# The last phase of a seven-product down projection divided in two, with late tiles from a ring of their own

## The chip, the cores and the metric

The kernel runs on one core of a Trainium2 chip. A core has five engines that run their own instruction lists and meet by semaphores: TensorE (PE, matrix products), VectorE (DVE), ScalarE (ACT), GpSimd (POOL) and SyncE (SP, which here only issues transfers). Sixteen DMA engines move data. The metric is the device time of one launch in microseconds (us).

## The reference, cut to what matters

One decoder layer on 512 tokens of width 1024, in fp32: two causal attention branches on a modulated input, merged by gates, an output projection and a layer norm, then a gated feed-forward part with a causal convolution of width 3 and a second layer norm.

```python
mod = c @ w_ada + b_ada
sh1, sc1, gt1, sh2, sc2, gt2 = [m[:, None, :] for m in jnp.split(mod, N_MOD, axis=-1)]
u = x * (1.0 + sc1) + sh1
proj = u @ w_in                      # q, k, v of both branches, forget logits, two gates
...
merged = jax.nn.sigmoid(g_a) * (y_fox @ w_fox_proj) + jax.nn.sigmoid(g_b) * (y_sb @ w_sb_proj)
x = _layer_norm(DEEPNORM_ALPHA * x + (1.0 + gt1) * (merged @ w_o), ln1_g, ln1_b)
u2 = x * (1.0 + sc2) + sh2
h = _causal_depthwise_conv(u2 @ w_up, conv_w, conv_b)      # 1024 -> 2 x 2816
h_gate, h_val = jnp.split(h, 2, axis=-1)
ffn_out = (jax.nn.silu(h_gate) * h_val) @ w_down           # 2816 -> 1024
x = _layer_norm(DEEPNORM_ALPHA * x + (1.0 + gt2) * ffn_out, ln2_g, ln2_b)
```

## The kernel before, in words

**Arithmetic.** Each fp32 product is three matmuls: weights and activations are split into a high half (rounded, by ScalarE, `hi_of`) and a low half (the rest, by VectorE, `lo_of`, the helper line L88), and high x high, high x low and low x high are added in a PSUM bank (`mm3`, L126 to L128, and `product`, L1040 to L1042). There are eight banks of 128x512.

**Weights.** A list `items` holds every weight tile in the order of use. `weights(i)` issues loads in this order on SP into a ring `raw` of five tiles of 128x1024, and calls the splitting of an item two ahead of its use. SP's list is in program order, so a load that waits for a free tile or for data holds up all loads behind it. The order of the other engines' lists is set by a scheduler from the program's order and its own estimate of when things are ready. Tiles that are kept for long (activations' halves `hv`, held weights `wdh`, `wdl`) come from a ring `z` of 58 tiles of 128x512.

**Before the feed-forward part.** While attention and merge run, the modulation vectors that are still missing are made on the side (`add_ada`, a tile of `w_ada` or `w_ct` at a time: the operations `ac` on VectorE, `raw,modr<-raw,cbc` and a reduction). The tiles of the output projection are scaled by `gt1` on GpSimd (L617). Then the output projection runs block by block (four blocks of 128 tokens): matmuls, the norm (`o_norm`, with a load of the input rows into `xn`, L874) and four transposes per block (`o_turn`, L902).

**The up-projection** has 44 column groups `n` of 128 columns, 24 matmuls each; each group is evacuated by ScalarE and VectorE through the convolution (`cv`). Two groups of gate and two of value make a pair `p`; there are eleven pairs.

**The down projection** splits tokens in two halves (blocks 0, 1 and blocks 2, 3), the 2816 rows into pairs, and the 1024 columns in two, and forms the four quadrants from seven products instead of eight, with sums of weight blocks and of activation blocks. Three products per pair (Y, Z2, P1; `early_products`, 18 matmuls) run while the up-projection goes on; for them `pair_proc` adds weight blocks, one addition by an accumulating transfer on the GpSimd queue (L148). One such sum is written to DRAM (`t13`) by the ScalarE queue, to be read again later. The other four products run behind the up-projection over all pairs: phase Z (right half of `t13`), phase V (left half), and a last phase with X (weights B21, columns 1536 to 2047 of the packed pair) and W (weights B22 times 1 + gate, columns 1024 to 1535). Combinations of the banks, a product with the gate (`gated`, L1113, L1114), and the second layer norm follow (`tail`: statistics, first pass L1128, second pass L1132, output).

**The last phase before:** for pairs 0 to 4, X and W take turns from one tile of 128x1024. The last six pairs (LATE = 6) have held tiles: scaled B22, written to DRAM as `wgt` between groups 36 and 41 (`scale_proc`), and B21, loaded together into a tile of the `raw` ring in phases Z and V and split into four held tiles. Blocks 0 and 1 are normed while X and W of the other blocks run (`first_rows`), then block 2, then block 3 in two pieces of 256 columns. The rows of the second norm's scale and shift are loaded on the GpSimd queue in phase V.

Of the kernel before, what the change touches and what calls it, by code (L numbers as in the profile page):

```python
# [8 lines left out]
F32 = mybir.dt.float32  # L9
F32R = mybir.dt.float32r  # L10
BF16 = mybir.dt.bfloat16
# [5 lines left out]
P = 128  # L17
# [22 lines left out]
LATE = 6  # L40
EARLY = 2
GS = 9
# [7 lines left out]
def layer_kernel(ctx: ExitStack, tc: tile.TileContext, out, xT, x, cT, crow, wa0, wa1, bcol, bgt, w1, wct, wv, bf,  # L50
# [7 lines left out]
    wgt = [tc.dram_tile([P, 512], F32, name=f"wgt_{q}") for q in range(LATE)]  # L58
    stg = ctx.enter_context(tc.tile_pool(name="stg", bufs=1))
    pp = ctx.enter_context(tc.tile_pool(name="pp", bufs=8, space=PSUM))  # L60
    zp = ctx.enter_context(tc.tile_pool(name="zp", bufs=1))
    st0 = ExitStack()
# [27 lines left out]
    cbc = const([P, D], F32, "cbc")  # L90
# [18 lines left out]
    identb = const([P, P], BF16, "identb")  # L109
    V.tensor_copy(identb, ident)  # L110
    zerob = const([P, P], BF16, "zerob")
    G.memset(zerob, 0.0)
    mska = const([P, P], BF16, "mska")
    G.affine_select(mska, zerob, pattern=[[-1, P]], compare_op=ALU.is_ge, fill=NEG, base=0, channel_multiplier=1)
    dg = const([P, 512], F32, "dg")
# [22 lines left out]
    def weights(i, ahead=AHEAD):  # L138
        while state["load"] < min(len(items), i + LOADS):
            it = items[state["load"]]  # L140
            it[3] = stg.tile([P, 1024], F32, name=nm("raw"), tag="raw", bufs=LOADS)
            c = 0
            for src in it[0] if isinstance(it[0], list) else [it[0]]:
                w = src.shape[-1]
                nc.sync.dma_start(it[3][:, c : c + w], src)
# [481 lines left out]
    def scale_proc(q):  # L627
        def f(r):
            V.tensor_tensor(r[:, 0:512], r[:, 0:512], gt[1][:, 512:1024], ALU.mult)
            G.dma_start(wgt[q], r[:, 0:512])  # L630
        return f

# [186 lines left out]
    fill(1 << 30)  # L819
    st2.close()  # L820


    st3 = ExitStack()
# [103 lines left out]
    def pair_proc(p):  # L927
        def f(r):
            b = items[pi[p][0]][4]
            V.tensor_tensor(r[:, 0:512], r[:, 0:512], b[:, 0:512], ALU.add)  # L930
# [9 lines left out]
    def add_pair_items(p):  # L940
        pi.append([add_item(wdp[p][:, 0:1024], raw_proc)])
        items[-1].append(wdp[p][:, 512:1536])
        pi[p].append(add_item(wdp[p][:, 0:512], halves_proc, 512))
# [4 lines left out]
    for n in range(2 * FT):  # L948
        wui.append(add_item(wup[n], split_proc))
        if n >= 5 and n % 4 == 1 and n < 2 * FT - 2:  # L950
            add_pair_items((n - 5) // 4)
        if n >= 6 and n % 4 == 2:
            add_pair_sums((n - 6) // 4)
        if 0 <= n - 2 * FT + LATE + 2 < LATE:
            q = n - 2 * FT + LATE + 2
            add_item(wdp[FP - LATE + q][:, 1024:1536], scale_proc(q), 512)
    zi, vi, cli, ci = [], [], [], []

    def add_late():
        if len(cli) < LATE:  # L960
            q = len(cli)
            cli.append(add_item([wgt[q], wdp[FP - LATE + q][:, 1536:2048]], wdc_proc))

    for n, half in (zi, 512), (vi, 0):
        for p in range(0, FP, 2):
            ws = [t13[q][:, half : half + 512] for q in range(p, min(p + 2, FP))]
            n.append(add_item(ws, split_cols(512 * len(ws)), 512 * len(ws)))
            if half and p == 2:
                add_pair_items(FP - 1)
                add_pair_sums(FP - 1)  # L970
            if not half or p == 8:
                add_late()
    for p in range(FP - LATE):
        ci.append(add_item(wdp[p][:, 1024:2048], split_proc))
# [7 lines left out]
    weights(last_wo, 0)  # L982
# [79 lines left out]
    hc = []  # L1062
    for n in range(2 * FT):
        if n < NSPLIT:
            h, l = items[wui[n]][4]
            ps = bks[n]
            up_mm(ps, h, l, slice(256, 512))
        else:
            ps = bank()
            h, l = weights(wui[n], min(LOADS - 1, wui[min(n + 2, 2 * FT - 1)] - wui[n]))  # L1070
            up_mm(ps, h, l, slice(0, 512))
            if n % 2 == 0 and 6 <= n < 22:
                o_x1((n - 6) // 4, n // 2 % 2 == 0)
            if n >= 7 and n % 4 == 3:
                early_products((n - 7) // 4)
            if n in (3, 4):
                list(ada_split(n + 3, 0))
            if n in (4, 5):
                list(ada_sum(n + 2))
# [23 lines left out]
    def fine(s):  # L1103
        return fin.tile([P, 512], F32, name=nm(s), tag="fz", bufs=12)

    r = x1
# [9 lines left out]

    wc = {}
# [19 lines left out]
    def t_phase(ps, idx, half, mark):  # L1137
        for n, k in enumerate(idx):
            w = weights(k)
            for p in range(2 * n, 2 * n + 2):  # L1140
                if half == 0 and GS <= p < FP:
                    ready(p)
            for a in range(2):
                p = 2 * n + a
                if p < FP:
                    t = ops[p][2][half]
                    for i in range(2):
                        m = product(ps[i], t[:, top[i]], t[:, bot[i]], *([v[:, a * 512 : (a + 1) * 512] for v in w]), p == 0, p == FP - 1)
                    ops[p][2][half] = None
            mark(n, m)  # L1150

    def z_mark(n, m):
# [3 lines left out]
        if n == 2:  # L1156
            early_products(FP - 1)
            Y, Z2, P1 = yz
# [5 lines left out]
        if n in (3, 4):  # L1164
            gated(n - 1, 0, p1[n - 3], p1[n - 3])

    def v_mark(n, m):
# [8 lines left out]
        if n == 2:  # L1176
            for i in range(2):
                t = fin.tile([P, D], F32, name=f"ln2_{i}", tag=f"ln2_{i}")
                paced(G.dma_start(t, lnrow[2 + i : 3 + i, :].broadcast_to([P, D])), m)
                lnr.append(t)  # L1180
        if n == 5:
            S.activation(lnr[0], lnr[0], AF.Copy, scale=-0.5)

    lnr = []
    Z = [bank() for _ in range(2)]
    t_phase(Z, zi, 0, z_mark)
    W = [bank() for _ in range(2)]
    t_phase(W, vi, 1, v_mark)
    for i in range(2):
        V.tensor_tensor(c22[i], u3[i], W[i], ALU.add)  # L1190
        V.tensor_tensor(u2[i], u2[i], W[i], ALU.add)
    for i in range(2):
        gated(i, 1, c22[i], c22[i], ALU.subtract)
    X, W = [[bank() for _ in range(2)] for _ in range(2)]
# [7 lines left out]
    for p in range(FP - LATE):  # L1202
        o, sp = ops[p][1], ops[p][3]
        w = weights(ci[p])
        for i in range(2):
            product(X[i], o[:, top[i]], o[:, bot[i]], *half(w, 1), p == 0, False)
        for i in range(2):
            product(W[i], sp[:, top[i]], sp[:, bot[i]], *half(w, 0), p == 0, p == FP - LATE - 1)
        if p % 2 == 0 and p < 4:
            first_rows(p // 2)  # L1210
    for q in range(LATE):
        wc[q] = weights(cli[q])
    for i in range(2):
        V.tensor_tensor(u2[i], W[i], u2[i], ALU.subtract)
        gated(2 + i, 1, u2[i], u2[i])
    for i in range(2):
        st = stat_tile()
        pieces = [(0, 0, 512), (1, 0, 512)] if i == 0 else [(0, 0, 512), (1, 0, 256), (1, 256, 512)]
        for n, (e, c0, c1) in enumerate(pieces):
            ps = bank()[:, 0 : c1 - c0] if e else X[i]  # L1220
            for q in range(LATE):
                t = ops[FP - LATE + q][3 if e else 1]
                product(ps, t[:, top[i]], t[:, bot[i]], wc[q][0][1 - e][:, c0:c1], wc[q][1][1 - e][:, c0:c1], e == 1 and q == 0, q == LATE - 1)
            v = r[2 + i][e][:, c0:c1]
            if e:
                V.tensor_tensor(v, v, ps, ALU.add)
            else:
                gated(2 + i, 0, p1[i], ps)
            V.bn_stats(st[:, n, :], v)
        tail(2 + i, st, pieces, nc.sync)  # L1230
# [71 lines left out]
```

## Time and profile before

| | us |
|---|---|
| runs shown | 765.49, 765.67, 760.73 (median 765.49) |
| the profiled execution | 761.97 |
| its span, first to last instruction | 760.2 |
| PE busy in the span | 736.8 |
| VectorE busy | 608.6 |
| ScalarE busy | 382.9 |
| up-projection, 420 to 640: PE busy | 220.00 of 220 |
| phases Z, V, X and W, 674 to 752: PE waits | 6.2 |
| from PE's last matmul to the end of the span | 8.4 |

How to read it: times are microseconds from the span's start. A line such as `L88 DVE ... wl<-raw,wh` names the line of the kernel, the engine, the operation and the tile written and read, without buffer numbers. `[0.76 <-DVE wl L88]` or "PE ps L1041 <- DVE wl L88: 5.8, 7, 1.2" tells that PE's instruction of line 1041 waited for VectorE's of line 88, 5.8 us in total, seven times, 1.2 at most. Durations overlap a little: the start of the next instruction is the better measure of what one costs. The granted clock was 0.995.

### The profile page before, as it was taken

How to read it: one execution, taken by the hardware profiler on the slowest of the kernel's cores; microseconds unless marked ns; L12 is line 12 of the kernel's file. 1: busy time of each engine (PE TensorE's matmuls, PEld its weight loads, DVE VectorE, ACT ScalarE, POOL GpSimd, SP SyncE). 2: the span in 40 equal slices, each digit the busy share in tenths (PEclk: the TensorE clock that was granted, in tenths of full speed). 3: DMA queues.
4: the chain of work that ended last, by engine and by line, in shares of the span. 5: the costliest groups of instructions: out<-in, count | busy, mean ns of one | idle time of the engine just before them, and what ended most of it. 6: DMA issues, size and time to landing. Idle time of an engine off the chain costs nothing.

```text
span 760.2 us, 9892 instructions
## 1 busy us (share of the span) xinstructions
PE 736.8 (97%) x3472; PEld 608.6 (80%) x3472; DVE 608.6 (80%) x1016; ACT 382.9 (50%) x679; POOL 113.7 (15%) x144
## 2 busy tenths in 40 slices
PE   8999999989999999999999999999999999999795
PEld 4878888867888887888889888888888888887574
DVE  6869799888898799666576999776867777679797
ACT  4567466675876564335045644543455344446520
POOL 1035223343000012453000000000000000000010
PEclk9999999999999999999999999999999999999998
DMA  8954446334532255435052656654764576767812
GB/s 332 405 193 132 173 173 216 111 112 139 167 121 76 84 166 193 145 111 191 3 152 84 207 183 192 208 142 157 210 186 139 170 213 221 226 179 258 278 53 77
DMA packets 42564, 128.80 MB, mean 169 GB/s; under 512 B 5617, under 2 KB 6129, under 8 KB 42514
## 3 DMA queue, kind: packets, MB, share of 16 engines
q1 hardware_dynamic: 37458, 112.61, 44.3%
q0 software_dynamic: 3184, 9.51, 5.8%
q10 hardware_dynamic: 1872, 6.05, 2.1%
q8 instruction: 27, 0.44, 0.2%
q14 instruction: 23, 0.19, 0.1%
HBM read 118.64 MB, written 9.44 MB: 168 GB/s over the span
## 4 chain that ended last, share of the span: by engine, by line
PE 71%; DVE 15%; DMA 6%; issue 4%; ACT 3%; DVEq 0%; SPq 0%; ACTq 0%
PE ps L126 15%; PE ps L127 15%; PE ps L128 15%; PE ps L286 5%; DVE wl L88 3%; PE ps L1041 3%; PE ps L1042 3%; PE ps L1040 3%; PE ps L880 2%; PE ps L881 2%; PE ps L879 2%; DMA raw<-in_wa 2%; DVE ac L571 2%; DVE om L498 2%; DVE raw L186 1%
## 5 line engine op out<-in xcount | busy, mean ns | idle before, releaser
L168 ACT ACTIVATE wh<-raw 128x1024 fp32r<-128x1024 f32 (+1 forms) x102 | 107.0, 1050 | 145.8 <-PE ps L127 97.9
L88 DVE TENSOR_TENSOR wl<-raw,wh 128x1024 fp32r<-128x1024 f32 (+2 forms) x111 | 132.5, 1195 | 42.0 <-ACT wh L168 41.7
L126 PE MATMUL ps<-u2h,wh 128*128 128x512 f32 (+1 forms) x376 | 141.5, 376 | 0.1
L128 PE MATMUL ps<-u2h,wl 128*128 128x512 f32 (+1 forms) x376 | 141.2, 376 | 0.0
L127 PE MATMUL ps<-u2l,wh 128*128 128x512 f32 (+1 forms) x376 | 141.2, 376 | 0.0
L126 PEld LDWEIGHTS ps<-u2h,wh 128*128 128x128 f32 x376 | 70.8, 188 | 13.2 <-issue 0.5
L127 PEld LDWEIGHTS ps<-u2l,wh 128*128 128x128 f32 x376 | 70.8, 188 | 12.9
L128 PEld LDWEIGHTS ps<-u2h,wl 128*128 128x128 f32 x376 | 70.8, 188 | 12.7
L126 PE MATMUL ps<-uh,wh 128*128 128x512 f32 x200 | 79.5, 397 | 0.0
L127 PE MATMUL ps<-ul,wh 128*128 128x512 f32 x200 | 78.2, 391 | 0.0
L128 PE MATMUL ps<-uh,wl 128*128 128x512 f32 x200 | 78.1, 390 | 0.0
L148 POOL DMA_DIRECT2D raw<-in_wdp x11 | 9.6, 870 | 248.8 <-DMA raw<-in_wdp 151.9
L128 PEld LDWEIGHTS ps<-uh,wl 128*128 128x128 f32 x200 | 37.6, 188 | 8.2
L499 POOL TENSOR_TENSOR pt<-pt,om 128x127 f32<-128x127 f32 (+3 forms) x32 | 42.7, 1346 | 9.4 <-DVE om L498 9.4
L126 PEld LDWEIGHTS ps<-uh,wh 128*128 128x128 f32 x200 | 37.6, 188 | 7.3
L127 PEld LDWEIGHTS ps<-ul,wh 128*128 128x128 f32 x200 | 37.7, 188 | 7.1
L1082 ACT ACTIVATE cv<-ps,cw 128x512 f32<-128x512 f32 x44 | 33.6, 764 | 7.2 <-PE ps L128 3.9
L1083 DVE SCALAR_TENSOR_TENSOR cv<-ps,cw,cv 128x511 f32<-128x511 f32 x44 | 32.8, 745 | 4.0 <-ACT cv L1082 3.9
L88 DVE TENSOR_TENSOR wdl<-raw,wdh 128x512 fp32r<-128x512 f32 x45 | 30.8, 687 | 6.0 <-ACT wdh L638 5.9
L1084 DVE SCALAR_TENSOR_TENSOR cv<-ps,cw,cv 128x510 f32<-128x510 f32 x44 | 32.8, 746 | 0.5
L617 POOL TENSOR_TENSOR raw<-raw,gt 128x1024 f32<-128x1024 f32 x8 | 20.7, 2590 | 79.7 <-DMA raw<-in_wo 74.2
L1090 ACT ACTIVATE cv<-cv 128x512 f32<-128x512 f32 x22 | 13.9, 633 | 36.4 <-DVE cv L1084 34.9
(223 smaller groups left out, 1621.3 us busy)
## 6 DMA issues: line engine op xcount, KB each, us to landing
raw<-in_wup SPq DMA_DIRECT2D x44, 512.0 KB, 3.5
raw<-in_wa SPq DMA_DIRECT2D x32, 512.0 KB, 3.9
raw<-in_wdp SPq DMA_DIRECT2D x27, 512.0 KB, 4.9
raw<-in_wct SPq DMA_DIRECT2D x25, 512.0 KB, 3.3
wa<-in_wa SPq DMA_DIRECT2D x14, 512.0 KB, 7.9
raw<-in_wdp SPq DMA_DIRECT2D x23, 256.0 KB, 4.9
raw<-in_wdp POOLq DMA_DIRECT2D x11, 512.0 KB, 6.6
t<-raw ACTq DMA_DIRECT2D x11, 512.0 KB, 5.1
```

Source lines behind the costliest of these rows:

```text
L88: return V.tensor_tensor(o, i, fl(hi), ALU.subtract)
L126: PE.matmul(ps, wh, ah, start=first, stop=False)
L127: PE.matmul(ps, wh, al, start=False, stop=False)
L128: return PE.matmul(ps, wl, ah, start=False, stop=last)
L168: state["hi"] = S.activation(h[:, 0:cols], r[:, 0:cols], AF.Copy)
L286: PE.matmul(grp[g], w, u, start=j == 0 and n == 0, stop=j == KT - 1 and n == (1 if g == 7 else 2))
L499: G.tensor_tensor(pt[b][:, s : e - 1], pt[b][:, s : e - 1], om[:, s + 1 : e], ALU.mult)
L1040: PE.matmul(ps, ah, bh, start=first, stop=False)
L1041: PE.matmul(ps, ah, bl, start=False, stop=False)
L1082: S.activation(t, ps, AF.Identity, bias=cw[:, n, 3:4], scale=cw[:, n, 2:3])
L1083: V.scalar_tensor_tensor(t[:, 1:], ps[:, 0:511], cw[:, n, 1:2], t[:, 1:], ALU.mult, ALU.add)
L1084: V.scalar_tensor_tensor(t[:, 2:], ps[:, 0:510], cw[:, n, 0:1], t[:, 2:], ALU.mult, ALU.add)
```

## The change

- **The last phase is two phases.** X (B21) runs for all eleven pairs as a phase of its own, two pairs to a tile of 128x1024, loaded from the weights. Then W (B22) runs: three pairs from tiles of `wgt`, then eight held pairs (LATE = 8).
- **All of B22 is scaled in the up-projection.** `pair_proc` multiplies it by the gate into a tile `wg` (VectorE) and writes it to DRAM on the ScalarE queue. `scale_proc` is gone.
- **Held tiles have their own ring:** the eight late tiles of `wgt` load into a ring `rl` of four tiles of 128x512, and the loads are spread over phases V and X.
- **Statistics earlier:** the result of X for blocks 2 and 3 is gated and added as W begins, and the statistics of its columns are taken there.
- **The second norm's rows** are loaded by SP at group 24, and one is scaled at group 28.
- **Modulation tiles:** in the merge, `add_ada` runs for j of 3 and above in the one list and for every j in the other, so the last ones come later; the sums of groups 6 and 7 are done at n = 3 and 4.
- **The first loads of the up-projection:** `weights(last_wo, 0)` is called ahead of the point where the up-projection's items are added to the list.
- Some constants move into a pool that closes after the merge, and Z's combinations come one step later.

```diff
-LATE = 6
+LATE = 8
...
+            if it[2] == 512:
+                it[3] = state["late"].tile([P, 512], F32, name=nm("rl"), tag="rl", bufs=4)
+            else:
+                it[3] = stg.tile([P, 1024], F32, name=nm("raw"), tag="raw", bufs=LOADS)
...
-            add_ada()
+            if j >= 3:
+                add_ada()
...
         add_bproj(0, j, merge(j))
+        add_ada()
...
     fill(1 << 30)
+    weights(last_wo, 0)
...
             b = items[pi[p][0]][4]
+            g = z(F32, "wg")
+            V.tensor_tensor(g, r[:, 0:512], gt[1][:, 512:1024], ALU.mult)
...
                 S.dma_start(t13[p], b)
+                S.dma_start(wgt[p], g)
...
+    for p in range(0, FP, 2):
+        add_two(vi, lambda q: t13[q][:, 0:512], p, FP)
+        if p > 2:
+            add_late()
+    for p in range(0, FP, 2):
+        add_two(xi, lambda q: wdp[q][:, 1536:2048], p, FP)
+        if p < 8:
+            add_late()
+    for p in range(0, FP - LATE, 2):
+        add_two(wi, lambda q: wgt[q], p, FP - LATE)
...
-    for p in range(FP - LATE):
-        o, sp = ops[p][1], ops[p][3]
-        w = weights(ci[p])
-        for i in range(2):
-            product(X[i], o[:, top[i]], o[:, bot[i]], *half(w, 1), p == 0, False)
-        for i in range(2):
-            product(W[i], sp[:, top[i]], sp[:, bot[i]], *half(w, 0), p == 0, p == FP - LATE - 1)
...
+    X = [bank() for _ in range(2)]
+    phase(X, xi, FP, lambda p: ops[p][1], x_mark)
+    W = [bank() for _ in range(2)]
...
+    for n, k in enumerate(wi):
+        w = weights(k)
+        for a, p in enumerate(range(2 * n, min(FP - LATE, 2 * n + 2))):
+            t = ops[p][3]
+            for i in range(2):
+                product(W[i], t[:, top[i]], t[:, bot[i]], *half(w, a), p == 0, i == 1 and p == FP - LATE - 1)
+        w_mark(n)
+    wc = [weights(k) for k in cli]
+    V.tensor_tensor(r[3][1], r[3][1], W[1], ALU.add)
...
+        pieces = [(1, 0, 512)] if i == 0 else [(1, 0, 256), (1, 256, 512)]
         for n, (e, c0, c1) in enumerate(pieces):
-            ps = bank()[:, 0 : c1 - c0] if e else X[i]
+            ps = bank()[:, 0 : c1 - c0] if i else W[0]
             for q in range(LATE):
-                t = ops[FP - LATE + q][3 if e else 1]
```

How the lists of the engines move is seen at three places. The first is SP's list where the up-projection begins, before (`in_wup` are its weights, `xn` the input rows of the four blocks):

```order
L863 DMA cw<-in_cwb 128x176
L145 DMA raw_3503<-in_wup 128x1024
...
L145 DMA raw_3509<-in_wup 128x1024
L874 DMA xn_3520<-in_x 128x512
...
L874 DMA xn_3773<-in_x 128x512
L145 DMA raw_3864<-in_wup 128x1024
```

And the same place now:

```order
L870 DMA cw<-in_cwb 128x176
L881 DMA xn_3524<-in_x 128x512
...
L881 DMA xn_3777<-in_x 128x512
L153 DMA raw_3868<-in_wup 128x1024
...
L153 DMA raw_3876<-in_wup 128x1024
```

The four loads that stood ahead of the eight `xn` loads stand behind them.

The second is PE's list at its very end, now (`ps_6830` is the bank of block 2 in the right half of the columns, `ps_6831` and the half-width `ps_6900` and `ps_6927` belong to block 3; `wdh`, `wdl` are held weights):

```order
L1053 MATMUL ps_6831<-wh_6820,hv_4704 128x512
L1053 MATMUL ps_6900<-wdh_6542,hv_4921 128x256
...
L1054 MATMUL ps_6927<-wdl_6716,hv_6205 128x256
L1054 MATMUL ps_6830<-wl_6821,hv_4704 128x512
...
L1055 MATMUL ps_6830<-wdh_6742,hv_6649 128x512
L1055 MATMUL ps_6927<-wdh_6715,hv_6205 128x256
L1053 MATMUL ps_6927<-wdh_6742,hv_6649 128x256
L1054 MATMUL ps_6927<-wdl_6743,hv_6649 128x256
L1055 MATMUL ps_6927<-wdh_6742,hv_6649 128x256
```

Before, the list ended with all 36 half-width matmuls of block 3 (18 into `ps_6883`, 18 into `ps_6904`), and block 2 was done ahead of them. Now 44 of 48 half-width ones come first, then 28 full ones, of which 26 go to block 2, then the last four.

The third is VectorE's list in the X phase, now, at the last low half of weights (`wl_6821`, for the third tile of W):

```order
L1136 TENSOR_TENSOR xn_3661<-xn_3661,u_1172_6314 128x512
L1152 SCALAR_TENSOR_TENSOR xn_3560<-xn_3560,mv_6803,ln_1_5287 128x512
L1152 SCALAR_TENSOR_TENSOR xn_3561<-xn_3561,mv_6803,ln_1_5287 128x512
L1135 TENSOR_TENSOR u_1173_6315<-u_1173_6315,gt_4175 128x512
L90 TENSOR_TENSOR wl_6821<-raw_6778,wh_6820 128x512
L1136 TENSOR_TENSOR xn_3777<-xn_3777,u_1173_6315 128x512
L1232 TENSOR_TENSOR p_1170_6312<-p_1170_6312,ps_6652 128x512
```

Before, the last low half stood ahead of the first pass of block 0's norm:

```order
L841 BN_AGGR mv_6714<-st_6711 128x2
L88 TENSOR_TENSOR wl_6744<-raw_6693,wh_6743 128x1024
L844 TENSOR_SCALAR mv_6714<-mv_6714 128x1
L1128 SCALAR_TENSOR_TENSOR xn_3520<-xn_3520,mv_6714,ln_0_6598 128x512
L845 RECIPROCAL mv_6714<-mv_6714 128x1
```

It now stands behind both blocks' norm passes.

More of the change, by code (lines that the diff above doesn't have):

```diff
@@ L57, in layer_kernel @@
     t13 = [tc.dram_tile([P, 1024], F32, name=f"t13_{p}") for p in range(FP)]
[L58 removed]
+    wgt = [tc.dram_tile([P, 512], F32, name=f"wgt_{q}") for q in range(FP)]
+    st1 = ExitStack()
     stg = ctx.enter_context(tc.tile_pool(name="stg", bufs=1))
@@ L953, in layer_kernel, with add_two @@
             add_pair_sums((n - 6) // 4)
[L954 to L957, printed above, removed]
+    zi, vi, xi, cli, wi = [], [], [], [], []
     def add_late():
         if len(cli) < LATE:
[L961 to L972, printed above, removed]
-    for p in range(FP - LATE):
-        ci.append(add_item(wdp[p][:, 1024:2048], split_proc))
+            cli.append(add_item(wgt[FP - LATE + len(cli)], halves_proc, 512))
+    def add_two(n, src, p, end):
+        ws = [src(q) for q in range(p, min(p + 2, end))]
+        n.append(add_item(ws, split_cols(512 * len(ws))))
+    for p in range(0, FP, 2):
+        add_two(zi, lambda q: t13[q][:, 512:1024], p, FP)
+        if p == 0:
+            add_pair_items(FP - 1)
+            add_pair_sums(FP - 1)
+    for p in range(0, FP, 2):
+        add_two(vi, lambda q: t13[q][:, 0:512], p, FP)
+        if p > 2:
+            add_late()
+    for p in range(0, FP, 2):
+        add_two(xi, lambda q: wdp[q][:, 1536:2048], p, FP)
[3 more added lines that the diff above has]
+        add_two(wi, lambda q: wgt[q], p, FP - LATE)
     def up_mm(ps, h, l, ts):
@@ L1103, in fine @@
     def fine(s):
-        return fin.tile([P, 512], F32, name=nm(s), tag="fz", bufs=12)
+        return fin.tile([P, 512], F32, name=nm(s), tag="fz", bufs=10)
+    state["late"] = fin
     r = x1
@@ L1135, in layer_kernel, with phase, g_part, f @@
     p1, u2, q1, u3, c22 = [[fine(n) for _ in range(2)] for n in ("p1", "u2", "q1", "u3", "c22")]
-    def t_phase(ps, idx, half, mark):
+    def phase(ps, idx, end, take, mark):
         for n, k in enumerate(idx):
             w = weights(k)
[L1140 to L1146, printed above, removed]
-                    for i in range(2):
[L1148 to L1152, printed above, removed]
+            for a, p in enumerate(range(2 * n, min(end, 2 * n + 2))):
+                t = take(p)
+                for i in range(2):
+                    product(ps[i], t[:, top[i]], t[:, bot[i]], *half(w, a), p == 0, p == FP - 1)
+            mark(n)
+    def g_part(c):
+        def f(p):
+            t = ops[p][2][c]
+            ops[p][2][c] = None
+            return t
+        return f
+    def z_mark(n):
         if n < 2:
@@ L1163, in z_mark, with v_mark @@
                 V.tensor_tensor(q1[i], u2[i], Z2[i], ALU.add)
-        if n in (3, 4):
-            gated(n - 1, 0, p1[n - 3], p1[n - 3])
-    def v_mark(n, m):
+        if n < 5:
+            for p in range(max(GS, 2 * n + 2), min(FP, 2 * n + 4)):
+                ready(p)
+    def v_mark(n):
         for p in range(max(SS, 2 * n), min(FP, 2 * n + 2)):
@@ L1213, in layer_kernel, with x_mark @@
-    for i in range(2):
[L1214 to L1218, printed above, removed]
+    def x_mark(n):
+        if n == 0:
+            for i in range(2):
+                V.tensor_tensor(c22[i], u3[i], W1[i], ALU.add)
+                V.tensor_tensor(u2[i], u2[i], W1[i], ALU.add)
+        if n in (1, 2):
+            gated(n - 1, 1, c22[n - 1], c22[n - 1], ALU.subtract)
+        if n in (3, 4):
+            first_rows(n - 3)
+        if n == 4:
+            for i in range(2):
+                gated(2 + i, 1, u2[i], u2[i], ALU.subtract)
@@ new lines, in layer_kernel, with w_mark @@
+    lnr = lnr2
+    Z = [bank() for _ in range(2)]
+    phase(Z, zi, FP, g_part(0), z_mark)
+    W1 = [bank() for _ in range(2)]
+    phase(W1, vi, FP, g_part(1), v_mark)
+    X = [bank() for _ in range(2)]
+    phase(X, xi, FP, lambda p: ops[p][1], x_mark)
+    W = [bank() for _ in range(2)]
+    sts = [cons.tile([P, 3, 6], F32, name=nm("st"), tag="st4", bufs=2) for _ in range(2)]
+    def w_mark(n):
+        if n == 0:
+            for i in range(2):
+                V.tensor_tensor(p1[i], p1[i], X[i], ALU.add)
+                gated(2 + i, 0, p1[i], p1[i])
+                V.bn_stats(sts[i][:, 0, :], r[2 + i][0])
@@ L1224, in layer_kernel @@
             v = r[2 + i][e][:, c0:c1]
[L1225 to L1230, printed above, removed]
+            V.tensor_tensor(v, v, ps, ALU.add)
+            V.bn_stats(sts[i][:, n + 1, :], v)
+        tail(2 + i, sts[i], [(0, 0, 512)] + pieces, nc.sync)
 def _pack(inputs):
```

71 lines of the change are left out of this document (27 added, 44 removed).

## The prediction

> **What bounds the kernel now.** I read the page first, then the stretches of the span, then the waits of TensorE, and at last the timeline of the last microseconds.
>
> ```profile
> PE 736.8 (97%) x3472; PEld 608.6 (80%) x3472; DVE 608.6 (80%) x1016; ACT 382.9 (50%) x679; POOL 113.7 (15%) x144
> ```
>
> TensorE (PE) is busy for 736.8 of 760.2 us, so only 23.4 us of the span are open to a change of order; the matmuls themselves are the same in number but for a few. Where those 23.4 us lie is told by the stretches (columns: length, then busy time and count of PE, its weight loads, VectorE, ScalarE and GpSimd, the granted clock, the DMA share and GB/s):
>
> ```profile
> 420.00:640.00 220.00, 220.00 (x972) 182.04 (x971) 172.67 (x280) 103.93 (x178) 9.67 (x13) 1.00 0.61 182
> 695.00:700.00 5.00, 4.24 (x18) 2.99 (x17) 4.50 (x8) 3.65 (x7) 0.00 (x0) 1.00 0.99 365
> ...
> 705.00:710.00 5.00, 3.23 (x14) 2.23 (x13) 4.77 (x7) 3.62 (x6) 1.05 (x2) 1.00 0.67 218
> ...
> 715.00:720.00 5.00, 3.22 (x12) 1.79 (x10) 2.29 (x3) 4.11 (x7) 0.00 (x0) 1.00 0.95 325
> 720.00:725.00 5.00, 4.71 (x20) 3.86 (x21) 5.00 (x9) 2.77 (x3) 0.00 (x0) 1.00 0.49 163
> ...
> 730.00:750.00 20.00, 20.00 (x100) 16.89 (x99) 19.90 (x44) 0.89 (x3) 2.18 (x4) 1.00 0.14 54
> 750.00:760.20 10.20, 1.78 (x15) 1.58 (x14) 6.15 (x17) 0.29 (x1) 0.00 (x0) 0.77 0.29 104
> ```
>
> The up-projection (420 to 640) has no gap: 972 matmuls in 220 us, 0.227 us each. From 695 to 730, where the seven-product phases run, PE has holes, with DMA at 0.95 to 0.99 or VectorE full. From 751.8 on PE is done and 8.4 us of tail follow. The waits of PE say what ends the holes:
>
> ```profile
> PE ps L1041 <- DVE wl L88: 5.8, 7, 1.2
> ...
> PE ps L126 <- ACT yh L85: 1.5, 1, 1.5
> PE ps L519 <- DVE vv L88: 0.9, 1, 0.9
> ...
> PE ps L1042 <- DVE hv L88: 0.4, 1, 0.4
> ```
>
> The first and last are the seven-product phases: 6.2 us, by VectorE's low halves of weights. The chain names what made VectorE late twice:
>
> ```profile
> 700.42 4.73 DMA raw<-t
> ...
> 709.92 7.89 DMA raw<-in_wdp
> ```
>
> Loads for the late pairs crowd into the stretch of the V phase. The third and fourth waits, in the merge, are the only others near moved work.
>
> **The change, part by part.** The sum is made against the profiled execution: 761.97 us, a span of 760.2 and 1.8 around it. It stands 3.5 us under the median of the three runs (765.49) and 1.2 over the lowest.
>
> *The last phases, waits.* X now takes B21 alone for all pairs and W follows, and the eight late tiles load into a ring of their own, spread over V and X, instead of six tiles of double width crowded into V. So the transfers of 4.73 and 7.89 us should no longer be last, and the 6.2 us go. What is late next is VectorE itself:
>
> ```profile
> 741.29 0.69 DVE L1113 TENSOR_TENSOR p<-ps,gt 128x512 f32<-128x512 f32 x1
> 741.88 0.69 DVE L1113 TENSOR_TENSOR u<-u,gt 128x512 f32<-128x512 f32 x1
> ...
> L88 DVE TENSOR_TENSOR wl<-raw,wh 128x1024 fp32r<-128x1024 f32 x10 | 12.2, 1216 | 2.1 <-ACT wh L168 2.1
> ```
>
> An operation of 128x512 starts 0.60 us after the one ahead of it, one of 128x1024 takes about 1.2. In the changed order VectorE has, between the last bank of Z and the first of V, 7 of width 1024, 14 of 512 and one of 256: 8.4 + 8.4 + 0.4 = 17.2 us, while PE's V phase is 66 matmuls, 15.0 us. Between V's bank and the last low half, `wl_6821`, it has 4 of 1024, 19 of 512, 8 passes of the layer norm at 0.67 and ten small ones (1.1): 22.7 us, while PE has 80 full matmuls and 44 of half width, 18.2 + 5.3 = 23.5. Walking the two lists against each other, PE waits about 0.6 at the last pair of Z (its low half stands behind three combinations), 1.6 at the first pair of V (behind the evacuation of Z), and twice 0.3 in X: 2.8 us. No row of before shows this order, so I bound it: 1 us, if the first low half of V is ready by the time its bank clears, and 6.2, if VectorE stays as late as it was. I take 2.8.
>
> *The end.* This is what speaks against the gain.
>
> ```profile
> 394.92 0.28 PE L128 MATMUL ps<-u2h,wl 128*128 128x256 f32 x1
> 395.03 0.28 PE L126 MATMUL ps<-u2h,wh 128*128 128x256 f32 x1
> ...
> 744.29 0.68 DVE L1226 TENSOR_TENSOR xn<-xn,ps 128x512 f32<-128x512 f32 x1
> ...
> 748.89 1.41 DVE L1132 SCALAR_TENSOR_TENSOR xn<-xn,mv,ln 128x512 f32<-128x512 f32 x2
> ...
> 751.82 0.42 DVE L1226 TENSOR_TENSOR xn<-xn,ps 128x256 f32<-128x256 f32 x1
> ...
> 753.08 0.74 DVE L1128 SCALAR_TENSOR_TENSOR xn<-xn,mv,ln 128x512 f32<-128x512 f32 x1
> ...
> 754.91 1.54 DVE L1132 SCALAR_TENSOR_TENSOR xn<-xn,mv,ln 128x512 f32<-128x512 f32 x3
> ```
>
> Before, the row block 2 is added at 744.29 and normed by 750.3 while PE still works on 36 half-width matmuls (0.12 us each) for block 3; behind PE only block 3 is left, 751.82 to 756.45, 4.6 us, and 3.75 for the last output. In the changed order, 44 of block 3's 48 half-width matmuls stand ahead of the 24 full ones of block 2, and 4 behind. So both blocks end together, and one engine norms them one after the other: the add (0.6), its statistics (0.6), for block 3 an add and two statistics (1.3), two aggregations and the small steps (1.1), first passes (three at 0.66, two at 0.4: 2.8), second passes (2.9): 9.3 us from the end of the last full matmul, which is 0.5 ahead of PE's end. 8.8 behind PE's end instead of 4.6 or 4.7: **+4.1**. It could be 5 if VectorE enters it late, 3.5 if the small steps overlap more. The 6 full matmuls that become 12 of half width cost 0.1.
>
> *The merge.* Five modulation steps come about three positions later.
>
> ```profile
> 292.10 2.73 POOL L617 TENSOR_TENSOR raw<-raw,gt 128x1024 f32<-128x1024 f32 x1 [8.27 <-DMA raw<-in_wo]
> ...
> 292.48 2.90 DVE L571 SCALAR_TENSOR_TENSOR ac<-raw,cTs,ac 128x512 f32<-128x512 f32 x1
> ...
> 296.94 1.53 DVE L571 SCALAR_TENSOR_TENSOR ac<-raw,cTs,ac 128x512 f32<-128x512 f32 x2
> ```
>
> The 1.53 us of `ac` at 296.94 stood ahead of what PE waited 1.5 us for, and one modulation operation of 1.2 stood ahead of the 0.9. Both leave: up to -2.3. But GpSimd's scaling of a tile of the output weights now meets other operations of VectorE, and where it met `ac` that took 2.90 instead of about 0.75: up to +2.15 if the same meets `pl` or `ptc`. I take -1.0, within -2.3 and +1.2. The page "SBUF — State Buffer" of the Trainium skill (Who interferes with whom) says that a VectorE operation with two SBUF inputs contends with a GpSimd one that reads SBUF, and one with at most one SBUF input does not. The 2.90 agrees, since `ac` reads two; `pl` and `ptc` read one from PSUM, so by that rule the collision would cost them nothing, and this term would be -2.3.
>
> *The start of the up-projection.*
>
> ```profile
> 341.22 6.59 SPq L145 DMA_DIRECT2D raw<-in_wup  x4
> 354.69 30.36 SPq L874 DMA_DIRECT2D xn<-in_x  x8
> 385.11 0.90 SPq L145 DMA_DIRECT2D raw<-in_wup  x2
> ...
> 394.60 0.36 PE L126 MATMUL ps<-u2h,wh 128*128 128x256 f32 x1
> ```
>
> SP issues in order. Four up-projection tiles were issued at 341 to 348, ahead of the eight `xn` loads; now they stand behind them, and the last `xn` ends at 385.05 because it waits for a slot. So the first tile is issued about 385.1 and lands by 389 to 391 (the loads of this line in that stretch took 3.4 to 6.2 us); with 1.05 for the high and 1.2 for the low half it is ready at 391 to 393.5, against 394.60. The second and third are needed some 3 us later each. VectorE's and ScalarE's splits, which used to be done long before, now fall into the norm of the last `xn`. I take +0.5, from 0 to 3.
>
> *The up-projection.* Eleven products `wg` (0.6 each) replace six scalings, and each pair's products are set one group of 24 matmuls earlier.
>
> ```profile
> L930 DVE TENSOR_TENSOR raw<-raw,raw 128x512 f32<-128x512 f32 x1 | 0.7, 691 | 2.7 <-DMA raw<-in_wdp 2.7
> ...
> L88 DVE TENSOR_TENSOR wdl<-raw,wdh x2: 689/691/693, 506.5 to 507.5; 128x512 fp32r<-128x512 f32 x2
> L1041 PEld LDWEIGHTS ps<-wdl,hv x2: 188/188/188, 518.6 to 519.3; 128*128 128x128 f32 x2
> ```
>
> Around 500 the low halves of a pair were made at 506.5 to 508.2 and used at 518.6: over 10 us of slack, out of which the change takes the group's 5.45 us and some 3 us of `wg` and later issue. About 1.8 us are left by my count, so nothing is lost while VectorE (172.67 of 220 busy) keeps its place. I take 0, from 0 to 3.
>
> Sum: 761.97 - 6.2 + 2.8 + 4.1 + 0.1 - 1.0 + 0.5 = **762.3**. Two of the three runs shown lie 3.5 us over the profiled one; taking about half of that, the forecast is **764 us**. 1% (7.6 us) is about what a measurement of this kernel can tell from no change.
>
> **The rivals.**
>
> *The tail is paid, and everything else comes.* All of the 6.2 goes and both waits of the merge: 761.97 - 6.2 - 2.3 + 4.1 + 0.1 = 757.7, or 759 with a part of the runs' offset. For it: DMA was at 0.95 to 0.99 in just the stretches with holes. Against it: VectorE was at 5.00 of 5 at 720 to 725, and none of its work there is taken away.
>
> *The wait stays, only its place moves.* If VectorE rather than the loads was the cause, the holes of 6.2 us come back at the heads of V and X: 762.3 + 3.4 = 765.7, some 767 with the offset. For it: 17.2 us of VectorE on 15.0 of PE. Against it: 2.29 busy of 5 at 715 to 720, where it stood idle for loads.
>
> *Slower: the products come too early.* If in the up-projection a pair's low halves come more than the 1.8 us later than I count, PE waits in each of ten periods, and every microsecond beyond costs 10: with 1 us it is 762.3 + 10 = 772, with 2 it is 782. For it: the sum of a pair waited 2.7 us for its accumulating load in the row quoted, and that load now comes later. Against it: in 220 us PE had no gap, and the group ahead of the products is there to wait in.
>
> **How the numbers follow.** The forecast has 0.50 (its own range 760 to 768), the first rival 0.18, the second 0.18, the third 0.14. The spread of the unknown terms is from -6.2 + 1 + 3.5 - 2.3 = -4.0 to +9 with all bad ones at once, and the runs lie 5 us apart; so 757 to 772, which leaves out a part of the first rival and most of the third. Faster by over 1% (below 757.8): a third of the first rival, 0.06. Slower by over 1% (above 773.1): most of the third and a late start, 0.12. Within: 0.82.
>
> **What would show it.** In the changed profile: PE's waits for low halves in the seven-product phases should sum to 1 to 4 us, with the longest at V's first pair; two row blocks should be normed one after the other behind PE's last matmul, about 12.5 us from that to the end of the span; 420 to 640 should stay without a gap; the first up-projection matmul should come within 1 us of the end of the last transposes. A gap in each of the ten periods, a first tile that lands after 393, or a tail of 8 us would make the prediction wrong.

## The result, and the profile after

The changed kernel takes 766.29 us (median of 20 runs, 764.36 to 768.09) against 764.34 for the kernel before (20 runs, 760.73 to 770.65). The ratio is 1.0028, with a 95% interval of 1.0014 to 1.0041: slower by a little under 0.3%. The forecast was 764.0 with a range of 757 to 772 and stood 1.5 us under the median then known; the time lies in the range and went the other way.

The profiled execution took 765.17 us, its span 763.4 (before 761.97 and 760.2). PE's waits, first of the changed kernel (engine, line, what it waited for: total, times, longest):

```profile
PE ps L133 <- DVE wl L90: 2.7, 1, 2.7
PE ps L545 <- DVE m L90: 2.7, 1, 2.7
PE ps L469 <- DVE m L90: 2.6, 1, 2.6
...
PE ps L1054 <- DVE wl L90: 1.4, 3, 0.7
PE ps L527 <- DVE vv L90: 0.7, 1, 0.7
...
PE ps L1053 <- ACT wh L176: 0.4, 1, 0.4
```

The second line is nothing new; the kernel before has the same wait:

```profile
PE ps L537 <- DVE m L88: 2.8, 1, 2.8
```

The waits of the seven-product phases, 6.2 us before, are 1.8 (the lines 1053 and 1054). But two waits are new, 2.7 us (L133) and 2.6 us (L469), and neither is in these phases: they stand in the merge and the attention. The stretches of the changed kernel show the same (length; PE, weight loads, VectorE, ScalarE, GpSimd busy; clock; DMA share; GB/s):

```profile
320.00:340.00 20.00, 17.85 (x71) 14.58 (x72) 14.91 (x15) 7.25 (x10) 9.84 (x5) 0.91 0.66 215
...
420.00:640.00 220.00, 220.00 (x972) 181.97 (x971) 174.88 (x284) 104.81 (x176) 6.88 (x8) 1.00 0.60 190
...
700.00:705.00 5.00, 4.22 (x15) 2.21 (x13) 4.72 (x8) 2.74 (x5) 0.00 (x0) 1.00 0.86 256
705.00:710.00 5.00, 4.42 (x19) 3.68 (x20) 3.71 (x5) 3.13 (x4) 0.00 (x0) 1.00 1.00 352
710.00:715.00 5.00, 5.00 (x23) 4.13 (x22) 5.00 (x8) 3.83 (x6) 0.00 (x0) 1.00 1.06 381
...
730.00:750.00 20.00, 20.00 (x109) 17.19 (x109) 20.00 (x41) 3.76 (x6) 2.21 (x4) 1.00 0.14 54
750.00:763.40 13.40, 1.83 (x11) 1.40 (x9) 9.79 (x27) 0.59 (x2) 0.00 (x0) 0.74 0.22 79
```

The up-projection is as full as before, VectorE is busy without a break from 710 to 750, and it has 9.79 us to do behind 750, where it had 6.15. With the starts of the first matmul of each stage, from the timelines of PE, the difference can be laid out. Z starts behind the products of pair 9 in both.

| us | before | after | difference |
|---|---|---|---|
| output projection starts | 348.51 | 353.38 | +4.87 |
| up-projection starts | 394.60 | 399.50 | +4.90 |
| phase Z starts | 678.11 | 683.06 | +4.95 |
| PE's last matmul ends | 751.78 | 751.83 | +0.05 |
| span ends | 760.2 | 763.4 | +3.2 |

So the profiled pair reads: +4.9 up to the output projection, nothing in the output projection and up-projection, -4.9 in the last phases, +3.15 in the tail. The gain that was looked for in the last phases came, and more than was looked for (4.9, where the terms of the sum give 3.3); a loss of the same size came where the prediction had a small gain, and the tail makes the rest.

### The profile page after: what moved, and what is told of

The parts are those of the page before. It is cut to its first block, busy times and chain, and to the rows that moved or that the text cites. A ratio compares the mean times of both kernels' runs of the same rounds, so it can differ in the third digit from the quotient of the medians.

```text
span 763.4 us, 9879 instructions
## 1 busy us (share of the span) xinstructions
PE 738.1 (97%) x3478; PEld 609.1 (80%) x3478; DVE 610.4 (80%) x1017; ACT 385.3 (50%) x678; POOL 107.0 (14%) x136
## 4 chain that ended last, share of the span: by engine, by line
PE 73%; DVE 14%; DMA 5%; issue 4%; ACT 3%; SPq 1%; POOL 0%; DVEq 0%; ACTq 0%; POOLq 0%
PE ps L133 15%; PE ps L131 15%; PE ps L132 15%; PE ps L294 4%; PE ps L1054 4%; PE ps L1055 4%; PE ps L1053 4%; DVE wl L90 3%; DMA raw<-in_wa 2%; PE ps L887 2%; PE ps L886 2%; PE ps L888 2%; DVE om L506 2%; PE ps L527 1%; DVE raw L194 1%
## 5 line engine op out<-in xcount | busy, mean ns | idle before, releaser
L90 DVE TENSOR_TENSOR wl<-raw,wh 128x1024 fp32r<-128x1024 f32 (+2 forms) x114 | 136.1, 1194 | 60.2 <-ACT wh L176 60.0
L176 ACT ACTIVATE wh<-raw 128x1024 fp32r<-128x1024 f32 (+1 forms) x105 | 109.7, 1045 | 133.5 <-PE ps L132 90.4
L133 PE MATMUL ps<-u2h,wl 128*128 128x512 f32 (+1 forms) x376 | 141.5, 376 | 0.0
L133 PE MATMUL ps<-uh,wl 128*128 128x512 f32 x200 | 79.0, 395 | 2.7 <-DVE wl L90 2.7
L133 PEld LDWEIGHTS ps<-u2h,wl 128*128 128x128 f32 x376 | 70.8, 188 | 12.9
L132 PE MATMUL ps<-ul,wh 128*128 128x512 f32 x200 | 78.9, 395 | 0.0
L133 PEld LDWEIGHTS ps<-uh,wl 128*128 128x128 f32 x200 | 37.9, 190 | 11.5 <-DVE wl L90 3.1
L1054 PE MATMUL ps<-wl,hv 128*128 128x512 f32 x72 | 28.7, 398 | 1.4 <-DVE wl L90 1.4
```

The lines of the kernel that those rows point to most:

```text
L90: return V.tensor_tensor(o, i, fl(hi), ALU.subtract)
L132: PE.matmul(ps, wh, al, start=False, stop=False)
L133: return PE.matmul(ps, wl, ah, start=False, stop=last)
L176: state["hi"] = S.activation(h[:, 0:cols], r[:, 0:cols], AF.Copy)
L1054: PE.matmul(ps, ah, bl, start=False, stop=False)
```

## The experiments

**The modulation tiles put back.** The changed kernel with only this edit:

```diff
-            if j >= 3:
-                add_ada()
+            add_ada()
...
         add_bproj(0, j, merge(j))
-        add_ada()
```

> The changed kernel with the modulation tiles back in their old places, nothing else. Theory (the modulation tiles cost the time): up to the output projection VectorE's list is that of before, so the output projection begins at 348.5 again instead of 353.4, the waits of 2.57 us at 214.8 and 2.72 at 322 are gone, the 1.47 at 301.6 is back, and the time falls by 4.9 us against the changed kernel, to about 0.998 of before. Rival (something else in the change costs it, such as the pool that closes early or the end phases): the waits stay, 1.003.

Measured: 762.25 us against 765.23, ratio 0.9962 (0.9939 to 0.9985). The output projection began at 348.57. The waits of 2.6 and 2.7 at the lines 469 and 133 are absent, and the one for `yh` is back, at 1.1:

```profile
PE ps L131 <- ACT yh L87: 1.1, 1, 1.1
```

So the rest of the change is worth 0.4%, and the moved modulation tiles cost 0.66% (from 0.9962 to 1.0028), 5 us.

**The same move alone, in the kernel before** (the same lines the other way round).

> The kernel before with the modulation tiles moved, nothing else. Theory: the output projection begins 4.9 us later, with both waits, and the time is 1.0064 of before. Rival: no more than 1.001.

Measured: 770.26 against 765.23, ratio 1.0070 (1.0045 to 1.0094). Both waits are there (the kernel's lines 461 and 128):

```profile
PE ps L461 <- DVE m L88: 3.2, 1, 3.2
...
PE ps L128 <- DVE wl L88: 2.8, 1, 2.8
```

In the profiled execution, of 772.94 us, the output projection begins 7.5 us later than in the profile of the kernel before, more than the 4.9 that were expected, and the clock is lower in the last phases too (0.91 from 695 to 710), so I take the size from the medians. The move costs some 5 us in either kernel.

**One half of the move undone.**

```diff
-            if j >= 3:
-                add_ada()
+            add_ada()
```

> The changed kernel with one half of the move undone: no modulation tile is left out for j below 3, those behind each product of the other branch stay. Theory (the wait at 214.8 comes from a modulation tile that loads later because of the first half, the one at 322 from the second half's tiles in the merge): the first wait is gone, about 1.6 us; the second gets smaller or goes, since the tiles are used up three places earlier, so 2 to 5 us less than the changed kernel. Rival (both waits belong to the second half): both stay.

Measured: 762.59 against 763.77, ratio 0.9978 (0.9957 to 0.9999), 3.8 us less than the changed kernel's ratio gives. Both waits are gone. So the half that leaves out three tiles early is what costs: it puts off all later modulation tiles, and with them what meets what in the merge. The loads show the shift. Before, SP issued three tiles of `w_ada` between 182 and 193:

```profile
182.10 5.66 SPq L145 DMA_DIRECT2D raw<-in_wa  x2
...
192.37 0.33 SPq L145 DMA_DIRECT2D raw<-in_wa  x1
```

In the changed kernel it issued none of them between these two:

```profile
176.63 0.33 SPq L153 DMA_DIRECT2D raw<-in_wa  x1
...
197.40 0.33 SPq L153 DMA_DIRECT2D raw<-in_wa  x1
```

How the first wait comes about is read from VectorE's timeline of the changed kernel:

```profile
207.32 1.22 DVE L194 SCALAR_TENSOR_TENSOR raw<-raw,cbc 128x1024 f32<-128x1024 f32 x1 [2.59 <-DMA raw<-in_wa]
```

and SP's, where this is the last load issued ahead of it:

```profile
203.09 5.82 SPq L153 DMA_DIRECT2D raw<-in_wa  x2
```

VectorE stood 2.59 us at the head of its list for a modulation tile that nobody needed yet, and behind it stood the softmax and the decay factors (`s`, `m`), for which PE then waited 2.57 at 214.83. Before, VectorE did not wait for the tile at this place:

```profile
202.95 1.23 DVE L186 SCALAR_TENSOR_TENSOR raw<-raw,cbc 128x1024 f32<-128x1024 f32 x1
```

**The output weights scaled by VectorE instead of GpSimd**, in the changed kernel. In its merge, GpSimd and VectorE run thus:

```profile
314.38 2.62 POOL L625 TENSOR_TENSOR raw<-raw,gt 128x1024 f32<-128x1024 f32 x1 [0.21 <-DMA raw<-in_wo]
317.33 2.47 POOL L625 TENSOR_TENSOR raw<-raw,gt 128x1024 f32<-128x1024 f32 x1 [0.34 <-ACT wh L176]
```

```profile
314.87 2.68 DVE L90 TENSOR_TENSOR ml<-sg,mh 128x512 fp32r<-128x512 f32 x1
317.47 2.89 DVE L579 SCALAR_TENSOR_TENSOR ac<-raw,cTs,ac 128x512 f32<-128x512 f32 x1
...
320.88 1.21 DVE L90 TENSOR_TENSOR wl<-raw,wh 128x1024 fp32r<-128x1024 f32 x1
```

PE got that `wl` at 322.15, 2.72 us late. The edit:

```diff
-        G.tensor_tensor(r, r, gt[0], ALU.mult)
+        V.tensor_tensor(r, r, gt[0], ALU.mult)
```

> The changed kernel with the output weights scaled by VectorE (1.2 us a tile) instead of GpSimd. Theory (the wait at 322 comes from GpSimd's scaling, beside which two operations of VectorE took 2.68 and 2.89 us instead of 0.69 and 0.75): the wait of 2.7 us and the lower clock behind it are gone, the output projection begins some 3 us earlier than in the changed kernel, the wait at 214.8 stays. Rival (the order of VectorE's list makes it): the wait stays, and the time is equal or longer.

Measured: 763.64 against 763.77, ratio 0.9995 (0.9971 to 1.0019). In its timeline the same operations take their own time, and PE waits 0.4 for that weight:

```profile
317.76 0.69 DVE L90 TENSOR_TENSOR ml<-sg,mh 128x512 fp32r<-128x512 f32 x1
318.37 0.74 DVE L579 SCALAR_TENSOR_TENSOR ac<-raw,cTs,ac 128x512 f32<-128x512 f32 x1
```

```profile
PE ps L469 <- DVE m L90: 3.7, 1, 3.7
...
PE ps L133 <- DVE wl L90: 0.4, 1, 0.4
```

The first wait stayed, longer in this execution (3.7). From the start of the branch projections to the output projection it takes 123.7 us, against 127.6 in the changed kernel and 124.3 before. So the second wait comes of GpSimd's scaling beside these operations: it goes when VectorE does the scaling, even though VectorE then has 1.2 us per tile more to do, and it is absent too where GpSimd scales as before but the tiles are back (the first and the third experiment). The intervals of the two medians overlap a little; the traces carry the verdict.

**Block 2 whole ahead of block 3 on TensorE,** in the changed kernel.

```diff
+                if i == 0:
+                    mlast = product(ps, ...)
+                else:
+                    with tc.issue_after(mlast.ins):
+                        product(ps, ...)
```

> The changed kernel with all 48 half-width matmuls of block 3 held behind the 24 full ones of block 2 on TensorE. Theory A (the order of TensorE makes the long tail): block 2 is normed while block 3 is multiplied, the tail falls from 11.7 to about 8.4 us and the time by 3 us. Theory B (VectorE's list, full from 710 us on, makes it): the last low half comes at 744.6, TensorE now waits for it some 5 us with nothing else to do, ends at about 756.8 instead of 751.7, and the time rises by 1 to 2 us against the changed kernel.

Measured: 770.56 against 765.23, ratio 1.0075 (1.0049 to 1.0102), slower than the changed kernel by almost 0.5%. PE waited for the last low half, and VectorE, full till then, for PE:

```profile
746.23 0.80 PE L1054 MATMUL ps<-wl,hv 128*128 128x512 f32 x1 [4.91 <-DVE wl L90]
```

```profile
755.28 0.69 DVE L1257 TENSOR_TENSOR xn<-xn,ps 128x512 f32<-128x512 f32 x1 [3.11 <-PE ps L1055]
```

It went as theory B has it, and cost more than it said (3.6 us by the ratios, where 1 to 2 were expected); the clock behind the 4.91 us wait was 0.60 over six microseconds, some 2.4 us lost. The tail behind PE did get shorter, 7.8 us instead of 11.6, but PE ended 9.2 us later. The half-width matmuls ahead of block 2 fill a wait for VectorE; to move them does not end the program earlier.

**Without the second norm pass of blocks 0 and 1,** in the changed kernel.

```diff
-            V.scalar_tensor_tensor(v, v, rs, lnr[1][:, c], ALU.mult, ALU.add)
+            if second:
+                V.scalar_tensor_tensor(v, v, rs, lnr[1][:, c], ALU.mult, ALU.add)
```

> The changed kernel without the second pass of the norm (scale by the deviation, add the shift) for blocks 0 and 1: it leaves out four operations of 0.7 us on VectorE ahead of the last low half. If VectorE alone sets the end, the time falls by 2.8 us. If TensorE's order and VectorE's list are tight at once (TensorE did not wait for the last low half, VectorE waited 0.38 us for TensorE), less than 0.5 us.

Measured: 764.76 against 765.23, ratio 1.0000 (0.9981 to 1.0019), 2.1 us less than the changed kernel by the ratios. That lies between my two figures, and both were made for a list of PE that stayed. It did not: with the last low half earlier, the scheduler set 21 half-width matmuls behind block 2 instead of 4, and the tail behind PE fell from 11.6 to 9.8, the way from the start of Z to the end of the span from 80.3 to 78.7. This run does not settle it.

**The norm of blocks 0 and 1 behind W's low halves,** with the modulation tiles back. The same work on each engine, in another order:

```diff
-        if n in (3, 4):
-            first_rows(n - 3)
...
                 V.bn_stats(sts[i][:, 0, :], r[2 + i][0])
+        first_rows(n)
```

> As the run with the modulation tiles back, and the norm of blocks 0 and 1 is set behind the low halves of W in VectorE's list. TensorE's list then has block 2 whole ahead of block 3's half-width matmuls, as in the kernel before, and the same work on every engine. Theory A (the late low half, and with it TensorE's order, makes the long tail): the tail falls from 11.9 to about 8.4 us and the time by 2 to 3 us against the run with the modulation tiles back. Theory B (VectorE is full from 710 us to the end whatever the order): within 0.5 us of it.

Measured: 761.15 against 763.77, ratio 0.9964 (0.9942 to 0.9985): the same as with the modulation tiles back alone (0.9962). PE's list now has block 2 whole, then block 3's 48 half-width matmuls, as it was before, and the tail behind PE is still 11.7 us. Its stretches show why:

```profile
710.00:730.00 20.00, 20.00 (x87) 15.71 (x86) 20.00 (x29) 10.37 (x14) 0.00 (x0) 1.00 0.61 199
730.00:750.00 20.00, 17.64 (x101) 15.41 (x99) 19.93 (x46) 2.80 (x5) 2.21 (x4) 1.00 0.14 53
```

VectorE (the third pair of numbers) is full for 40 us. PE is done at 747.6 and VectorE carries on alone. Theory A falls.

**Without the second pass, in that order.** The last two edits together.

> As the run with the modulation tiles back and the norm of blocks 0 and 1 set later, without the second pass of that norm: it leaves out four operations of VectorE, 2.75 us, and TensorE's list does not change with it. Theory B (VectorE is the bound from 710 us to the end): the time falls by 2 to 2.8 us against that run. Theory A (TensorE's end and a fixed tail behind it are the bound): no change.

Measured: 759.63 against 764.24, ratio 0.9939 (0.9916 to 0.9962). From the start of Z to the end of the span it is 78.9 us, against 80.7 with the pass. That is 1.8 less by the traces and 1.9 by the ratios, just under theory B's 2 to 2.8, and far from theory A's nothing; the intervals of the medians overlap by half, and the two traces agree with them. PE's list did stay as it was.

**The statistics of blocks 0 and 1 by ScalarE,** in that order and with the whole computation.

```diff
-        for e in range(2):
-            V.bn_stats(st[:, e, :], r[i][e])
...
+        for e in range(2):
+            j = z(F32, "junk")
+            S.activation(j, r[i][e], AF.Copy, scale=1.0 / D, accum_out=a[:, e : e + 1])
+            S.activation(j, r[i][e], AF.Square, scale=1.0 / 32, accum_out=a[:, 2 + e : 3 + e])
...
```

> As the run with the modulation tiles back and the norm of blocks 0 and 1 set later, with the whole computation, but the sums for the mean and the deviation of blocks 0 and 1 are made by ScalarE, which is idle for most of that stretch, instead of VectorE. Some 2.3 us of VectorE leave it (four statistics of 0.6 and two aggregations, against five small steps more). Theory B: 1.5 to 2.3 us less than that run, if ScalarE's sums don't hold up its high halves. Theory A: no change.

Measured: 759.87 against 764.24, ratio 0.9938 (0.9912 to 0.9963). Z to the end is 78.9 us again, 1.8 less than in the same order with the statistics on VectorE (2.0 by the ratios). The stretches (VectorE is the third pair of numbers):

```profile
710.00:730.00 20.00, 20.00 (x87) 15.81 (x86) 19.79 (x29) 12.99 (x23) 0.00 (x0) 1.00 0.64 208
730.00:750.00 20.00, 18.08 (x103) 15.75 (x101) 20.00 (x50) 4.91 (x13) 2.21 (x4) 1.00 0.14 53
750.00:764.00 14.00, 0.00 (x0) 0.00 (x0) 4.52 (x13) 0.29 (x1) 0.00 (x0) 0.65 0.21 76
```

It is still the full engine, with 4.52 us behind 750 where it had 5.77. This version beats both kernels: 0.6% under the kernel before, with the whole interval under 1.

**Three held tiles loaded in phase Z,** with the modulation tiles back.

```diff
             add_pair_sums(FP - 1)
+        if p > 4:
+            add_late()
```

> As the run with the modulation tiles back, with three of the eight held tiles loaded and split in phase Z already, where VectorE has idle time (16.9 busy of 21 us at 674 to 695), instead of V and X. Theory B (VectorE's work from 710 on sets the end): 1.8 us of it leave that stretch, the time falls by 1 to 2 us against the run with the modulation tiles back. Rival (the earlier loads hold up Z and V on SP's queue): it rises.

Measured: 762.55 against 763.77, ratio 0.9970 (0.9946 to 0.9994), no gain on 0.9962. VectorE's stretch from 710 to 750 is a little less full (19.35 and 19.50 of 20), but PE waits a little more in Z and V (2.8 us against 2.5), and the clock there was 0.89 between 695 and 710. From Z to the end it is 81.2 us, against 81.1. What VectorE saved late was lost early; neither theory's figure came.

## Why the prediction was wrong

**The merge is the step that failed**, as the term for the moved modulation tiles. I gave it -1.0, within -2.3 and +1.2, and it was +4.9 in the profiled pair, 5 us by the medians. Of its working, half came: the 1.5 us wait for `yh` went, but the 0.9 only became 0.7 (0.7 to 1.3 where the tiles are back), and it stands at 190 us, in the attention and not in the merge, where I had it. Two things were missing. First, I followed the moved operations only where they had stood and not where their loads went: leaving out three tiles shifts every later one on SP's queue, and an operation that waits for its load at the head of VectorE's list holds up everything behind it. That cost the 2.57 us at 214.83. Second, I looked for GpSimd's scaling among `pl` and `ptc`, where one tile went; two others now stood beside `ml` and `ac`, and these took 2.68 and 2.89 us. That cost the 2.72 us at 322.15. The page "SBUF — State Buffer" of the Trainium skill (Who interferes with whom) names the kind rightly: both read two SBUF operands. The rule spoke for a smaller cost at the place where I applied it, and for a larger one at a place that I did not look at.

**The waits of the last phases.** 6.2 us should go and 2.8 come; 1.8 came, and PE needed 4.9 less from Z to its end (3.3 by my terms); the listed waits make 4.4 of it, the rest is open. The two list walks named most of the places: 0.6 at the last pair of Z, as taken, and the longest at the head of V, 0.7 where I took 1.6. The two of 0.3 that I had in X are not there; the last wait, 0.44 at 716.99, is at the ninth pair of V.

**The tail.** +4.1 against 3.15 measured, of about the right size and with the wrong cause. I put it down to the order of block 2 and block 3 on PE. What I counted on VectorE's list behind the last full matmul is there (9.3 us taken, 8.8 in the trace), but it would be as late with another order: with that of before, the tail stayed at 11.7 us, and from there 2.75 us less of VectorE's work, or 2.3 moved to ScalarE, shortened the way from Z to the end by 1.8 each. VectorE has more work between 710 and the end than PE, and the order decides only on whose list the waiting shows. The loads that made VectorE idle before (2.3 of 5 us busy at 715 to 720) are gone, and so the same work is now done earlier, but by less than PE gained: from the start of Z, PE ends 4.9 us sooner and the span 1.8.

**The start of the up-projection**, +0.5: 46.12 us from the output projection to it, against 46.09. The late loads had room: the first tile landed at 394.8 and its low half was done at 397.1, ahead of the first matmul at 399.50. (A landing after 393 was named as a sign of being wrong; with the 4.9 us by which everything there came later it is 389.9, within the forecast.) **The up-projection**, 0: 0.05. Here the slack held, and the rival with ten gaps has nothing in the trace.

**From the sum to the forecast.** The sum of 762.3 was 0.3 over the profiled execution. I then added only half of the offset to the median of three runs, and so forecast a time under that median although the sum stood a little over its own base. With 20 runs the median of before is 764.34; the same sum, as a ratio, would have been 1.0004. The sign was lost here, independent of the step above.

Of the rivals, none is what happened: the waits did go, the products did not come too early, and the merge got worse instead of better. The time lies in the range because the range was wide, not because the mechanism was right: the merge missed by 5.9 us, and the last phases, the tail and the start of the up-projection, each better than its term, took back 3.0. None of the signs that I named looks at the merge; the waits of 1.8, the full up-projection and a tail of 11.6 (12.5 named) came nearly as named, and the time went the other way.

## What to carry to other kernels

When a change shifts a list of transfers, follow every later entry: a late load costs at the first in-order engine that stands at its head, long before anything needs its result. A full engine hides behind the order of another one; test it by taking work away from it and by reordering, each alone, before calling a tail a matter of order. And a sum made against one profiled execution should be carried over as a ratio.

## What the runs showed of the hardware

A wait of PE of 2 to 3 us can cost more than itself. In the changed kernel behind the wait of 2.72 us:

```profile
322.20:324.00 1.80, 1.80 (x6) 1.47 (x7) 1.80 (x4) 0.34 (x1) 0.00 (x0) 0.72 0.84 244
324.00:326.00 2.00, 2.00 (x6) 1.52 (x6) 1.75 (x2) 0.83 (x2) 1.27 (x1) 0.50 0.98 375
326.00:328.00 2.00, 2.00 (x10) 1.60 (x9) 2.00 (x3) 1.56 (x3) 0.55 (x1) 0.90 0.89 309
328.00:330.00 2.00, 2.00 (x10) 1.68 (x9) 2.00 (x2) 1.12 (x2) 2.00 (x1) 1.00 0.81 217
```

The granted clock (third from the right) fell to 0.50 for some 3.4 us; 0.72 over the six microseconds from 322.2 is 1.7 us lost, on top of the 2.72. The wait of 2.57 at 214.8 in the same execution had no such dip. Another wait, at 160 us, stands in every profile with 2.5 to 2.8 us: it was followed by a dip in the kernel before (0.76 from 161 to 168), and by none in the changed kernel (1.00). Of the twelve profiles six have it, with no difference in the length of the wait that would tell them apart. Nor does it take one long wait. With block 2 held ahead of block 3, a wait of 2.11 us at 214.29 was followed by a clock of 0.57 from 215 to 219; with one half of the move undone, two short waits close together were followed by the same:

```profile
188.18 0.52 PE L527 MATMUL ps<-ident,pt 128*128 128x128 f32 x3 [1.09 <-DVE vv L90]
189.97 0.60 PE L527 MATMUL ps<-ident,pt 128*128 128x128 f32 x3 [1.27 <-DVE vv L90]
```

```profile
190.00:194.00 4.00, 4.00 (x13) 3.21 (x14) 4.00 (x11) 3.75 (x13) 0.00 (x0) 0.57 0.52 176
```

The page "TensorE: Matmul & The Clock Gate" of the Trainium skill (Part 1: The HAM clock gate) has half clock after at least one idle window of about 3.4 us, in a window that runs free. The dips of 0.50 agree with it in depth, and their chance nature with a free window; that waits of 2.7 us, shorter than the window, are enough does not. So 1.7 us of a single pair of profiles can be chance, which is as much as many terms of such a sum. In the pair compared here each kernel has one such dip ahead of the output projection, the kernel before at 161 and the changed one at 323, each worth about 1.7 us, so they cancel in the +4.9.
